# A causal matrix convolution: finishing a third of the outputs on ScalarE and GpSimd instead of VectorE

## The chip, the core and the metric

The kernel runs on one core of a Trainium2 chip. A core has five engines that run at once[...]: TensorE (PE, matmuls), VectorE (DVE), ScalarE (ACT), GpSimd (POOL) and SyncE (SP, which here only issues DMA). Matmul results land in PSUM; everything else lies in SBUF. The metric is the device time of one execution in microseconds (us).

## The reference

```python
B, S, D, K = 8, 4096, 512, 8
# x: [B, S, D] float32, kernel: [K, D, D] float32
out = 0
for k in range(K):
    shifted = x shifted down by k steps along S, zeros in front
    out += np.matmul(shifted, kernel[k])
```

Each output row is the sum of eight matrix products, of the row itself and its seven predecessors with eight 512 x 512 matrices.

## The kernel before

The 32768 rows are laid out as 128 runs (one on each partition) of 256 steps; an iteration handles 8 steps of every run, and there are 32. Within an iteration the kernel uses a fast (Karatsuba-like) scheme on the taps: three nodes, MID, LO and HI, each of nine 128 x 512 by 512 x 512 products. The MID node gives a common part `ms`, and the outputs of LO are its own sums plus `ms`, those of HI its own sums minus `ms`. Each node has two output tiles, b = 0 and 1, of 128 x 1024 float32 (two steps). The inputs of the products are sums of transposed inputs in bfloat16 (`XT`, `D1`, `D2`, `D21`, `D4`, `D41`, `D42`, `D421`), which VectorE prepares (`tt` is `nc.vector.tensor_tensor`). The engines' queues are taken in program order.

The helpers that matter here:

```python
def load(out, src):
    nc.gpsimd.dma_start(out=out, in_=src)          # float32 to bfloat16 on the way

def transpose_x(i, h):                             # half an iteration's input
    nc.sync.dma_start_transpose(out=XT[:, 4 * h:4 * h + 4, :]..., in_=xin[i, h]...)

def product(bank, comp, w, start):                 # four matmuls
    for c in range(DC):
        nc.tensor.matmul(bank, lhsT=comp[:, c * P:(c + 1) * P], rhs=w[:, c, :], ...)

mpool = tc.tile_pool(name="m", bufs=2)             # ms
ypool = tc.tile_pool(name="y", bufs=4)             # y
xpool = tc.tile_pool(name="x", bufs=2)             # xin

def node_a1(k): ...
    product(n.q[:, 1], ...)
    nc.scalar.copy(out=n.q[:, 0], in_=n.q[:, 1])                  # L244

def node_seed(n, b_):                                             # L256, L258
    n.p[b_] = pair((2 * n.k + b_) % 3)             # one of three PSUM pairs, in turn
    if b_ == LO: nc.scalar.copy(out=n.p[b_][:, 1], in_=n.q[:, 1])
    else:        nc.scalar.mul(out=n.p[b_][:, 1], in_=n.q[:, 1], mul=-1.0)

def node_dts(n): ...                                              # L262, ScalarE
def node_v(n, b_): product(n.p[b_][:, 1], ...)
def node_d(n, b_): ...            # VectorE: p[:, 0] from dts and p[:, 1]; L76, L272
def node_l(n, b_, j): product(n.p[b_][:, j], n.s[3][2 * b_ + j], W[n.a, b_, j], False)

def store(i, a, b_, y):
    nc.sync.dma_start(out=orr[:, t0:t0 + 2, :], in_=y)            # L282
```

The steady loop (the first six nodes are written out by hand; shown from the seventh on):

```python
for k, (i, a) in enumerate(order):            # (MID, LO, HI) of i = 2, 3, ... 31
    ...
    if a == MID and more: transpose_x(i + 1, 0)
    node_l(cur, 0, LO); node_l(cur, 0, HI)
    if nxt: node_a0(nxt); node_u(nxt)
    node_l(cur, 1, LO)
    node_e(cur, 0)                            # first output tile
    if nxt: node_seed(nxt, 0); node_seed(nxt, 1); node_dts(nxt)
    if a == MID:   prep_d421(LO); prep_d41(HI)
    elif a == LO:
        if more: prep_m()                     # reads the first half of the new XT
        prep_d421(HI)
    elif more:     prep_d41(LO); prep_d42(LO); prep_d21()
    if nxt:
        for b_ in range(2): node_v(nxt, b_); node_d(nxt, b_)
    if a == MID:   prep_d42(HI); prep_d27()
    elif more:     prep_d4(LO if a == LO else HI)     # HI: reads the second half of XT
    node_l(cur, 1, HI)
    if k + 2 < len(order): node_a1(k + 2)
    node_e(cur, 1)                            # second output tile
    if a == LO and more:
        transpose_x(i + 1, 1)
        if i + 2 < NIT: load_x(i + 2, 0); load_x(i + 2, 1)
```

Of the kernel before, what the change touches and what calls it, by code (L numbers as in the profile page):

```python
# [18 lines left out]
LO, HI, MID = 0, 1, 2  # L19
# [3 lines left out]
def kernel(  # L23
# [6 lines left out]
    nc = tc.nc  # L30
# [10 lines left out]
    ADD = mybir.AluOpType.add  # L41
    SUB = mybir.AluOpType.subtract
# [32 lines left out]
    def tt(o, a, b, op):  # L75
        nc.vector.tensor_tensor(out=o, in0=a, in1=b, op=op)  # L76
# [198 lines left out]
    ms = {}  # L275
# [4 lines left out]
    def store(i, a, b_, y):  # L280
        t0 = K * i + 4 * a + 2 * b_
        nc.sync.dma_start(out=orr[:, t0:t0 + 2, :], in_=y)  # L282
# [7 lines left out]
    def node_e(n, b_):  # L290
        p = n.p[b_]
        if n.k < 4:
            pool, name = ((mpool, "ms"), (ypool, "y"), (fpool, "f"), (ypool, "y"))[n.k]
            y = pool.tile([P, 2, D], f32, name=name)
            nc.scalar.copy(out=y, in_=p)  # L295
            first[n.i, n.a, b_] = y
        elif n.a == MID:
            ms[b_] = mpool.tile([P, 2, D], f32, name="ms")
            nc.scalar.copy(out=ms[b_], in_=p)  # L299
        else:  # L300
            y = ypool.tile([P, 2, D], f32, name="y")
            if b_ == HI and n.k == len(order) - 1:

                for j, eng in enumerate((nc.scalar, nc.sync)):
                    tt(y[:, j], p[:, j], ms[b_][:, j], ADD if n.a == LO else SUB)
                    eng.dma_start(out=orr[:, K * n.i + 4 * n.a + 2 * b_ + j, :], in_=y[:, j])
            else:
                tt(y, p, ms[b_], ADD if n.a == LO else SUB)
                store(n.i, n.a, b_, y)


# [108 lines left out]
    mid_dve(1, HI, HI)  # L420
    node_u(nodes[1])
    node_e(nodes[0], 0)
    prep_d27()
    mid_dve(2, HI, LO)
# [13 lines left out]
    mid_dve(2, HI, HI)  # L438
    mid_dve(2, HI, MID)
    node_e(nodes[0], 1)  # L440
    node_l(nodes[1], 0, HI)
    node_d(nodes[1], 1)
    prep_d421(HI)
    mid_acc(HI, LO)
    node_a1(2)
    node_l(nodes[1], 0, LO)
    node_e(nodes[1], 0)
    mid_dve(0, HI, HI)
    transpose_x(1, 1)
# [202 lines left out]
```

## Time and profile before

The median of two runs is 779.34 us (779.10 and 779.57). The profiled execution has a span of 777.3 us, with TensorE at its full granted clock throughout.

| engine | busy, us | share of span |
|---|---|---|
| TensorE matmuls | 766.8 | 99% |
| VectorE | 657.5 | 85% |
| ScalarE | 284.9 | 37% |
| GpSimd | 42.3 | 5% |

GpSimd's time is almost all issue of loads. The DMA queues of SyncE move 99.89 MB (stores and transposes), that of GpSimd 38.67 MB (loads).

In a group of instructions, the line reads: line of the kernel, engine, operation, what it writes and reads with shapes, count, then busy time in all, mean of one in ns, and the idle time of the engine just before with what ended it. `D` stands for all of the tiles D1 to D421, `pp` for the PSUM pairs. In a timeline a line begins with start and duration in us; neighbouring instructions of one kind are merged (x3), and `SPq` is a DMA issued from SyncE's queue. L76 is the helper `tt`, L89 the transpose, L80 the load.

### The profile page before, as it was taken

The page shows a single profiled execution, that of the slowest core. Times are in us where ns is not written, and L with a number is a line of the kernel's source. Part 1 is how long each engine was busy: PE and PEld are TensorE (multiplying, and loading weights), DVE is VectorE, ACT ScalarE, POOL GpSimd, SP SyncE. Part 2 cuts the span into 40 slices and gives each one's busy share as a digit, 9 for nine tenths or more (in the row PEclk, how much of TensorE's full clock was granted, in tenths as well). Part 3 has the DMA queues.
Part 4 walks back from the last instruction along what each step waited for, and adds up shares of the span by engine and source line. Part 5 has one row for each costly group of instructions (what it writes and reads, how often), then busy time and mean ns, then how long its engine had stood idle before and what let it go on. Part 6 is the DMA issues. An engine that isn't in the chain of part 4 may idle for free.

```text
span 777.3 us, 9450 instructions
## 1 busy us (share of the span) xinstructions
PE 766.8 (99%) x3584; PEld 347.3 (45%) x3584; DVE 657.5 (85%) x766; ACT 284.9 (37%) x462; POOL 42.3 (5%) x80
## 2 busy tenths in 40 slices
PE   7999999999999999999999999999999999999997
PEld 3444444444444444444444444444444444444443
DVE  4999988898888898888898888898888898888895
ACT  3553343333343333343333343333343333343332
POOL 4000000000000000000000000000000000000000
PEclk9999999999999999999999999999999999999999
DMA  9986878868786877787877878877697867687843
GB/s 199 211 125 170 226 185 178 208 159 190 164 199 163 197 172 189 164 198 169 194 171 187 164 174 190 207 162 188 163 187 176 207 158 190 165 186 179 204 133 121
DMA packets 159373, 139.42 MB, mean 179 GB/s; under 512 B 130144, under 2 KB 134240, under 8 KB 159200
## 3 DMA queue, kind: packets, MB, share of 16 engines
q1 hardware_dynamic: 145456, 99.89, 46.1%
q0 software_dynamic: 13728, 38.67, 31.6%
q8 instruction: 28, 0.46, 0.2%
q10 hardware_dynamic: 144, 0.26, 0.1%
q14 instruction: 17, 0.14, 0.1%
HBM read 77.33 MB, written 67.11 MB: 186 GB/s over the span
## 4 chain that ended last, share of the span: by engine, by line
PE 96%; DMA 2%; POOL 1%; ACT 0%; issue 0%; DVE 0%; DVEq 0%; POOLq 0%
PE pp L197 96%; DMA xin<-in_x_dram 2%; POOL w L80 0%; PE pp L186 0%; ACT y L295 0%; DVE y L76 0%; DVE pp L76 0%; POOL xin L80 0%; DVEq L647 0%; ACT pp L256 0%; ACT pp L244 0%; POOL XT L80 0%; PE pp L180 0%; POOL ident masks.py:199 0%; POOL ident masks.py:197 0%
## 5 line engine op out<-in xcount | busy, mean ns | idle before, releaser
L197 PE MATMUL pp<-w,D 128*128 128x512 bf16 x3280 | 715.5, 379 | 1.3 <-DVE w L76 0.9
L197 PEld LDWEIGHTS <-D 128*128 128x128 bf16 x3280 | 320.4, 98 | 389.8 <-issue 2.8
L76 DVE TENSOR_TENSOR D<-D 128x1024 bf16<-128x1024 bf16 (+1 forms) x252 | 228.2, 945 | 1.6 <-ACT D L353 1.6
L76 DVE TENSOR_TENSOR y<-pp,ms 128x1024 f32<-128x1024 f32 (+1 forms) x121 | 146.5, 1212 | 45.5 <-PE pp L197 45.4
L76 DVE TENSOR_TENSOR D<-XT 128x2048 bf16<-128x2048 bf16 (+2 forms) x153 | 142.1, 946 | 8.5 <-DMA XT<-xin 6.7
L244 ACT COPY pp<-pp 128x512 f32<-128x512 f32 x95 | 54.1, 570 | 256.0 <-PE pp L197 256.0
L256 ACT COPY pp<-pp 128x512 f32<-128x512 f32 x95 | 54.1, 570 | 170.6 <-PE pp L197 167.6
L76 DVE TENSOR_TENSOR pp<-dts,pp 128x512 f32<-128x512 f32 x95 | 65.5, 690 | 46.2 <-ACT dts L262 44.6
L299 ACT COPY ms<-pp 128x1024 f32<-128x1024 f32 x60 | 61.0, 1016 | 33.1 <-PE pp L197 33.1
L80 POOL DMA_DIRECT2D xin<-in_x_dram x64 | 34.2, 535 | 688.3 <-DMA XT<-xin 670.6
L272 DVE SCALAR_TENSOR_TENSOR pp<-pp,dts 128x512 f32<-128x512 f32 x95 | 65.9, 693 | 3.2
L262 ACT COPY dts<-pp 128x512 f32<-128x512 f32 x95 | 57.4, 604 | 2.0 <-PE pp L197 2.0
L258 ACT ACTIVATE pp<-pp 128x512 f32<-128x512 f32 x95 | 56.0, 589 | 1.2 <-DVE y L76 1.2
L197 PE MATMUL pp<-w,XT 128*128 128x512 bf16 x120 | 30.8, 379 | 0.0
L76 DVE TENSOR_TENSOR w<-w,w 128x2048 bf16<-128x2048 bf16 x18 | 21.6, 1219 | 0.4 <-DMA w<-in_kernel_dram 0.2
L197 PEld LDWEIGHTS <-XT 128*128 128x128 bf16 x120 | 11.7, 98 | 14.2
L180 PE MATMUL pp<-zero 128*128 128x512 bf16 x24 | 8.9, 505 | 2.4 <-DVE zero L145 1.2
L197 PE MATMUL pp<-w,w 128*128 128x512 bf16 x36 | 9.0, 379 | 1.3 <-ACT pp L244 0.7
L197 PE MATMUL pp<-w,F 128*128 128x512 bf16 x36 | 8.9, 379 | 0.0
L338 DVE MEMSET D<- 128x64 bf16 x2 | 0.2, 112 | 8.2 <-ACT D L351 7.7
L80 POOL DMA_DIRECT2D w<-in_kernel_dram x8 | 6.0, 766 | 0.8 <-DMA w<-in_kernel_dram 0.8
L197 PEld LDWEIGHTS <-w 128*128 128x128 bf16 x36 | 3.5, 97 | 5.8 <-issue 2.1
(55 smaller groups left out, 70.6 us busy)
## 6 DMA issues: line engine op xcount, KB each, us to landing
out_dram<-y SPq DMA_DIRECT2D x123, 512.0 KB, 3.5
xin<-in_x_dram POOLq DMA_DIRECT2D x64, 512.0 KB, 5.9
w<-in_kernel_dram POOLq DMA_DIRECT2D x8, 512.0 KB, 15.9
D<-in_x_dram SPq DMA_DIRECT2D x1, 1024.0 KB, 4.9
out_dram<-ms SPq DMA_DIRECT2D x2, 512.0 KB, 4.2
out_dram<-f SPq DMA_DIRECT2D x2, 512.0 KB, 3.7
XT<-xin SPq DMA_TRANSPOSE x61, 6.1
w<-w POOLq DMA_DIRECT2D x1, 512.0 KB, 9.9
```

The lines of the kernel that those rows point to most:

```text
L76: nc.vector.tensor_tensor(out=o, in0=a, in1=b, op=op)
L80: nc.gpsimd.dma_start(out=out, in_=src)
L180: nc.tensor.matmul(pw[:, h], lhsT=zero[:, 0:P], rhs=zero, start=True, stop=True)
L197: nc.tensor.matmul(bank, lhsT=comp[:, c * P:(c + 1) * P], rhs=w[:, c, :], start=start and c == 0, stop=c == DC - 1, skip_group_check=True)
L244: nc.scalar.copy(out=n.q[:, 0], in_=n.q[:, 1])
L256: nc.scalar.copy(out=n.p[b_][:, 1], in_=n.q[:, 1])
L258: nc.scalar.mul(out=n.p[b_][:, 1], in_=n.q[:, 1], mul=-1.0)
L262: nc.scalar.copy(out=n.dts, in_=n.q[:, 0])
L272: nc.vector.scalar_tensor_tensor(out=p[:, 0], in0=p[:, 1], scalar=-1.0, in1=n.dts, op0=MUL, op1=SUB)
L299: nc.scalar.copy(out=ms[b_], in_=p)
L338: nc.vector.memset(z[:, :, 0:D:G], 0.0)
```

## The change

The two outputs of every LO node no longer go through one VectorE addition that reads PSUM and writes SBUF. ScalarE copies the PSUM pair into the output tile, and GpSimd[...] adds `ms` to it in place. HI outputs stay on VectorE. The purpose is to take work off VectorE, the second busiest engine, and give it to two that have room; the sums are the same.

```diff
@@ node_e
                 for j, eng in enumerate((nc.scalar, nc.sync)):
                     tt(y[:, j], p[:, j], ms[b_][:, j], ADD if n.a == LO else SUB)
                     eng.dma_start(out=orr[:, K * n.i + 4 * n.a + 2 * b_ + j, :], in_=y[:, j])
+            elif n.a == LO:
+                nc.scalar.copy(out=y, in_=p)
+                nc.gpsimd.tensor_tensor(out=y, in0=y, in1=ms[b_], op=ADD)
+                store(n.i, n.a, b_, y)
             else:
-                tt(y, p, ms[b_], ADD if n.a == LO else SUB)
+                tt(y, p, ms[b_], SUB)
                 store(n.i, n.a, b_, y)
```

The order of work on TensorE and of issues on SyncE stays as it was. On GpSimd the two additions of a LO node come ahead of the two loads that are written after it.

## The prediction

> **What bounds the kernel now.** I read the page first: shares of busy time, then the chain of waits, then the groups. After that I read the timeline of one iteration in the steady part, because shares are averages over three different stages. The page, parts 1 and 4:
>
> ```profile
> PE 766.8 (99%) x3584; PEld 347.3 (45%) x3584; DVE 657.5 (85%) x766; ACT 284.9 (37%) x462; POOL 42.3 (5%) x80
> ...
> PE 96%; DMA 2%; POOL 1%; ACT 0%; issue 0%; DVE 0%; DVEq 0%; POOLq 0%
> ```
>
> TensorE is busy 99% and holds 96% of the chain. The detailed chain has one unbroken piece of 726.95 us and 3364 matmuls: 0.216 us each, 0.864 us for a product of four, 7.78 us for a node of nine products, 23.3 us for an iteration of MID, LO, HI. Every other engine works in its shadow, so taking work off VectorE buys nothing by itself; what counts is how much delay each helper may suffer before TensorE stops. The groups concerned, with shapes kept apart:
>
> ```profile
> L76 DVE TENSOR_TENSOR y<-pp,ms 128x1024 f32<-128x1024 f32 x119 | 145.2, 1221 | 45.0 <-PE pp L197 44.9
> L299 ACT COPY ms<-pp 128x1024 f32<-128x1024 f32 x60 | 61.0, 1016 | 33.1 <-PE pp L197 33.1
> ```
>
> Half of the first group moves; the second shows what a 128x1024 copy out of PSUM costs on ScalarE. Now the timeline of one iteration (start, duration, engine, line; in brackets the idle time before it). The LO node's products begin on TensorE at about 412.68: ScalarE's first seed (416.14) is released by the fourth product.
>
> ```profile
> 414.36 1.23 DVE L76 TENSOR_TENSOR y<-pp,ms 128x1024 f32<-128x1024 f32 x1 [1.29 <-PE pp L197]
> 414.60 0.53 POOL L80 DMA_DIRECT2D xin<-in_x_dram  x1 [9.46 <-DMA XT<-xin]
> ...
> 420.47 0.57 ACT L244 COPY pp<-pp 128x512 f32<-128x512 f32 x1 [2.75 <-PE pp L197]
> 420.70 1.22 DVE L76 TENSOR_TENSOR y<-pp,ms 128x1024 f32<-128x1024 f32 x1
> ...
> 422.38 3.26 SPq L89 DMA_TRANSPOSE XT<-xin  x1
> ...
> 423.28 2.95 DVE L76 TENSOR_TENSOR D<-D 128x1024 bf16<-128x1024 bf16 x3
> ...
> 426.15 0.69 DVE L76 TENSOR_TENSOR pp<-dts,pp 128x512 f32<-128x512 f32 x1
> ...
> 427.50 1.23 DVE L76 TENSOR_TENSOR D<-XT 128x2048 bf16<-128x2048 bf16 x1
> ...
> 428.64 1.22 DVE L76 TENSOR_TENSOR y<-pp,ms 128x1024 f32<-128x1024 f32 x1
> ...
> 431.63 0.57 ACT L256 COPY pp<-pp 128x512 f32<-128x512 f32 x1 [0.71 <-PE pp L197]
> ```
>
> 414.36 and 420.70 are the two outputs of LO. The transpose at 422.38 comes right after the second one's store, because the SyncE queue is taken in order. VectorE needs what it brings at 427.50 (prep_d4 of the upper half); behind that stands the second output of HI (428.64, done 429.86), which frees the PSUM pair that the seed at 431.63 overwrites. So the spare time in this line is 431.63 - 429.86 = 1.77 us. The kernel itself has tried it: at another iteration, where a transpose landed late,
>
> ```profile
> 242.67 1.23 DVE L76 TENSOR_TENSOR D<-XT 128x2048 bf16<-128x2048 bf16 x1 [1.79 <-DMA XT<-xin]
> ...
> 245.12 0.57 ACT L256 COPY pp<-pp 128x512 f32<-128x512 f32 x1 [0.76 <-PE pp L197]
> ```
>
> 1.79 us of delay reached VectorE and TensorE just did not stop. Anything beyond that is paid on the path.
>
> [...] The trace has no GpSimd arithmetic of this kind to compare; VectorE takes 1.22 us for the version that reads PSUM. [...] a transpose suffers beside a load: with no load near, the one issued at 422.38 had landed by 427.50 (5.1 us at most); the one issued at 407.06, 2.45 us after a load, released the next load only at 414.60 (7.5 us).
>
> **The change part by part.** It removes 60 VectorE additions (30 LO nodes with two outputs), 60 x 1.22 = 73 us, leaving about 584 us of VectorE. It adds 60 ScalarE copies of 1.016 us, 61 us, making 346 us (44%), and 60 GpSimd additions of an estimated 2.3 us, 138 us. Nothing moves on TensorE. The stores keep their places in the SyncE queue but now wait for GpSimd. The two loads of each iteration stand behind both GpSimd additions in GpSimd's own queue.
>
> ScalarE has room. The first copy runs at 414.4 to 415.4, before the seed of 416.14; the second after the copy of 420.47, from 421.0 to 422.0, before its next work at 423.86. PSUM is freed at 422.0 where it was 421.92. Nothing is lost here.
>
> GpSimd's second addition then runs 422.05 to 424.35 where VectorE had finished at 421.92: the LO output is complete 2.4 us later. Its store and the transpose behind it go with it: the transpose is issued at 424.8. At the same moment, 424.4, GpSimd issues the load that used to go at 414.60, so load and transpose now start together[...]. The transpose lands after 5.1 us if unhurt, at 429.9, and after some 7.5 us if it is slowed as above, at 432.3. VectorE's second HI output ends 2.36 us later (429.86 - 427.50 in the trace): 432.3 or 434.7. The seed takes 0.57 more and a semaphore, so the first v product of the next LO can start at 432.9 or 435.3; it was due at 412.68 + 7.78 + 7.78 + 5 products x 0.864 = 432.5. TensorE loses 0.4 or 2.8 us in each iteration. I take 2.4, since I expect the collision in most of them.
>
> The lock adds to that. The three D additions due at 423.28 wait for GpSimd until 424.4; node_d then ends at 428.0, and the MID node wants it at 428.2: it just fits. GpSimd's first addition (from 415.45) competes with prep_m and the D421 addition; as the other transpose is issued behind the delayed HI store, it lands later too, and GpSimd will often be first. Then 2.9 us of D additions and 0.7 us of node_d follow 417.8, to 421.4, where the HI node starts at 420.4: up to 1.0 us lost. I take 0.6.
>
> The sum is 2.4 + 0.6 = 3.0 us in each of 29 iterations that still load a successor (the last LO has no transpose behind it), 87 us. The saved VectorE time shortens nothing on the path. 779.3 + 87 = 866 us.
>
> **The rivals.** (a) Nothing changes: the 1.77 us of spare time swallow the delay, as in the late transpose above. This asks for an addition under 1.7 us or a transpose that is quicker than now; the estimates speak against it. It would give 775 to 790. (b) A gain through VectorE's relief: VectorE at 85% looks like a near bound, but TensorE's chain has no wait on it in the steady part, so at most the small start-up and end waits are in play, under 5 us, and those are not touched. (c) GpSimd itself becomes slow: if it often waits for the port behind VectorE's D additions, an addition lasts 4 to 5 us instead of 2.3, and the store, transpose and load go with it; each us more is about 29 us. That would give 900 to 950. (d) ScalarE as the bound: at 44%, with gaps at both places where the copies fall, I hold this unlikely; it would show as seeds that wait for a copy.
>
> **Range and chances.** With a clean transpose and no lock loss, 29 x 0.4 gives 791, and a slightly slow addition already passes 800. With the full collision and the full lock loss, 29 x 3.8 gives 890; with GpSimd delayed by half a us besides, 905. The range for 8 in 10 is 815 to 908. Slower by over 2% (above 795) needs 0.55 us lost in an iteration: 0.92. Within 2%: 0.07. Faster: 0.01.
>
> **What would show each step right or wrong.** TensorE's busy time should stay while its idle time grows by the loss, and its waits should name ScalarE's seeds (L256) in the MID nodes, which in turn wait for VectorE's HI output, and that for the DMA transpose: VectorE's wait on XT should grow from 6.7 us to well over 60. The stores of LO should wait for GpSimd, and the transposes after them land in 7 us or more. GpSimd's additions should last about 2.3 us each, in step with D additions that start late. I am wrong on the transpose if VectorE's wait on it stays small; wrong on the lock if D additions run during GpSimd's; wrong altogether if TensorE's chain stays unbroken.

## The result, and the profile after

The changed kernel takes 989.17 us (median of two, 987.74 and 990.61) against 779.34: a ratio of 1.269, interval 1.265 to 1.274. That is 209.8 us, or 7.2 us for each of the 29 iterations that transpose a successor's input in the LO node. The prediction said 866, with 908 at the top of its range. The outputs that moved are 60 of the 128 output tiles, so nearly half and not the third of the title. The page of the changed kernel, busy times, the clock granted to TensorE in 40 slices (tenths), and the chain by engine:

```profile
PE 830.8 (84%) x3513; PEld 362.0 (37%) x3584; DVE 636.6 (65%) x706; ACT 343.4 (35%) x522; POOL 192.7 (20%) x140
...
PEclk9999999998899888998888988889888898888989
...
PE 49%; DMA 30%; DVE 13%; issue 5%; ACT 2%; POOL 0%; another core or an unknown queue 0%; DVEq 0%; ACTq 0%; POOLq 0%
```

TensorE held 96% of the chain and now holds 49%; DMA has 30%. TensorE's busy time also grew, by 64.0 us, with the same matmuls to do, and its mean granted clock is 0.909. The waits (who waited for whom: us in all, times, longest):

```profile
DVE D L76 <- DMA XT<-xin: 185.1, 58, 6.9
ACT pp L256 <- DVE y L76: 159.8, 29, 6.8
PE pp L197 <- ACT pp L256: 135.6, 30, 6.1
```

The same three waits in the kernel before:

```profile
DVE D L76 <- DMA XT<-xin: 6.7, 6, 1.8
ACT pp L256 <- DVE y L76: 0.8, 1, 0.8
PE pp L197 <- ACT pp L256: 0.7, 1, 0.7
```

Read upwards: TensorE waits for the seed, the seed for VectorE's HI output, and VectorE for the transpose, 29 times or more each. The 135.6 us of waiting and the 64.0 us of slower matmuls make 199.6 of the 208.7 us by which the span grew (986.0 against 777.3). One iteration in the timeline:

```profile
510.46 0.15 PEld L197 LDWEIGHTS <-D 128*128 128x128 bf16 x1 [0.27 <-issue]
...
510.89 0.15 PEld L197 LDWEIGHTS <-D 128*128 128x128 bf16 x1 [0.28 <-issue]
511.32 0.15 PEld L197 LDWEIGHTS <-D 128*128 128x128 bf16 x1 [0.28 <-issue]
...
524.08 2.35 POOL L309 TENSOR_TENSOR y<-y,ms 128x1024 f32<-128x1024 f32 x1 [4.15 <-issue]
...
525.26 3.99 DVE L76 TENSOR_TENSOR D<-D 128x1024 bf16<-128x1024 bf16 x3
...
526.37 0.57 POOL L80 DMA_DIRECT2D xin<-in_x_dram  x1
...
526.96 6.88 SPq L89 DMA_TRANSPOSE XT<-xin  x1
...
537.35 1.23 DVE L76 TENSOR_TENSOR D<-XT 128x2048 bf16<-128x2048 bf16 x1 [6.89 <-DMA XT<-xin]
...
538.50 1.22 DVE L76 TENSOR_TENSOR y<-pp,ms 128x1024 f32<-128x1024 f32 x1
...
539.80 0.57 ACT L256 COPY pp<-pp 128x512 f32<-128x512 f32 x1 [6.83 <-DVE y L76]
...
540.42 15.70 PE L197 MATMUL pp<-w,D 128*128 128x512 bf16 x63 [5.97 <-ACT pp L256]
```

GpSimd's second addition ends at 526.43. Its load goes out at 526.37 and the transpose at 526.96, 0.59 us apart. The transpose brings its data after 10.3 us, where it was 5.1 before; VectorE waits 6.89 us, the seed goes at 539.80 and TensorE has stood still for 5.97 us. Of the 28 transposes of this place that have a load beside them, 19 landed in 8.6 to 9.0 us, three in 9.2 to 9.3 and six in 9.9 to 10.3; TensorE stood 4.1 to 4.8 us after the first 19 and up to 6.1 after the others. The first three lines show what follows such a gap: weight loads, one for each matmul, come every 0.43 us instead of every 0.216. The granted clock is 0.50 in the first 2 us of work after this gap (540.30 to 542.30) and 1.00 again from 544.30 on.

The groups of arithmetic on GpSimd and of VectorE's D additions, and the last of them in the kernel before:

```profile
L76 DVE TENSOR_TENSOR D<-D 128x2048 bf16<-128x2048 bf16 x123 | 158.0, 1303 | 0.0
L309 POOL TENSOR_TENSOR y<-y,ms 128x1024 f32<-128x1024 f32 x60 | 151.2, 2519 | 453.5 <-ACT y L308 343.4 <-issue 110.1
L76 DVE TENSOR_TENSOR D<-D 128x1024 bf16<-128x1024 bf16 x127 | 112.0, 921 | 1.6 <-ACT D L357 1.6
```

```profile
L76 DVE TENSOR_TENSOR D<-D 128x1024 bf16<-128x1024 bf16 x127 | 81.8, 682 | 1.6 <-ACT D L353 1.6
```

GpSimd's additions take 2.34 to 2.35 us where no D addition runs beside them (11 of the 60) and 2.52 us on average. VectorE's D additions of 128x1024 went from 682 to 921 ns. 29 of them began while a GpSimd addition was running: every one ended after it, and they took 1.37 to 2.00 us where the other 98 took 0.68 to 0.69. So the two exclude each other, and the time in which an instruction waits is counted as its own. The 28 HI outputs that began during a GpSimd addition, and read PSUM for one operand, did not wait: 1.22 to 1.23 us, where 29 others without one took 1.22. "Lock" and "port" in the recorded texts are names for this exclusion, and what lies behind it no run shows.

### The profile page after: what moved, and what is told of

Read it like the earlier page. It is cut to its first block, busy times and chain, and to the rows that moved or that the text cites. A ratio compares the mean times of both kernels' runs of the same rounds, so it can differ in the third digit from the quotient of the medians.

```text
span 986.0 us, 9495 instructions
## 1 busy us (share of the span) xinstructions
PE 830.8 (84%) x3513; PEld 362.0 (37%) x3584; DVE 636.6 (65%) x706; ACT 343.4 (35%) x522; POOL 192.7 (20%) x140
## 4 chain that ended last, share of the span: by engine, by line
PE 49%; DMA 30%; DVE 13%; issue 5%; ACT 2%; POOL 0%; another core or an unknown queue 0%; DVEq 0%; ACTq 0%; POOLq 0%
PE pp L197 49%; DMA XT<-xin 28%; DVE y L76 7%; DVE D L76 6%; DMA xin<-in_x_dram 2%; ACT pp L256 2%; POOL w L80 0%; DVE pp L76 0%; PE pp L186 0%; ACT y L295 0%; POOL xin L80 0%; DVEq L76 0%; DVEq L651 0%; ACT pp L244 0%
## 5 line engine op out<-in xcount | busy, mean ns | idle before, releaser
L197 PE MATMUL pp<-w,D 128*128 128x512 bf16 x3214 | 780.1, 402 | 142.0 <-ACT pp L256 135.0
L197 PEld LDWEIGHTS <-D 128*128 128x128 bf16 x3280 | 335.2, 102 | 580.9 <-issue 227.9
L76 DVE TENSOR_TENSOR D<-D 128x1024 bf16<-128x1024 bf16 (+1 forms) x252 | 269.3, 1108 | 1.6 <-ACT D L357 1.6
L76 DVE TENSOR_TENSOR D<-XT 128x2048 bf16<-128x2048 bf16 (+2 forms) x153 | 144.5, 961 | 185.1 <-DMA XT<-xin 185.1
L309 POOL TENSOR_TENSOR y<-y,ms 128x1024 f32<-128x1024 f32 x60 | 151.2, 2519 | 453.5 <-ACT y L308 343.4
L244 ACT COPY pp<-pp 128x512 f32<-128x512 f32 x95 | 54.1, 570 | 318.4 <-PE pp L197 310.2
L76 DVE TENSOR_TENSOR y<-pp,ms 128x1024 f32<-128x1024 f32 (+1 forms) x61 | 73.4, 1204 | 42.4 <-PE pp L197 40.8
L308 ACT COPY y<-pp 128x1024 f32<-128x1024 f32 x60 | 61.0, 1017 | 6.9 <-PE pp L197 6.7
```

The costliest lines, as they stand in the source:

```text
L309: nc.gpsimd.tensor_tensor(out=y, in0=y, in1=ms[b_], op=ADD)
```

## The experiments

Four theories. A, collision: the load, held back by GpSimd's additions, starts together with the transpose and slows it. B, queue: the transpose is issued late because it stands behind a store that waits for a slow addition. C, exclusion: VectorE's D additions and GpSimd's additions wait for each other, and that delay reaches TensorE. D, clock: after the gap TensorE runs at half speed. A ratio is always to the kernel before, measured on the same chip.

### Taking the collision away: the load goes first

```diff
+        if a == LO and i + 2 < NIT:
+            load_x(i + 2, 0)
         node_l(cur, 0, LO)
@@
             if i + 2 < NIT:
-                load_x(i + 2, 0)
                 load_x(i + 2, 1)
```

> The changed kernel, with the first of an iteration's two loads written ahead of the LO node's two GpSimd additions instead of behind them. Theory A (the load, held back by the additions, starts together with the transpose and slows it): the second-half transpose lands in 5 to 6 us again instead of about 10, TensorE loses at most 1 us an iteration and its clock stays full; 785 to 815 us. Theory B (the transpose is late because it stands behind a store that waits for a 2.5 us addition): nothing of that changes, the time stays above 900. Theory C[...]: above 900 too.

836.64 us, ratio 1.075 (1.072 to 1.077): 152.5 us of the 209.8 are gone by moving one load. The chain of waits of this run shows the second-half transposes (start, duration until it released the next step):

```profile
451.88 4.97 DMA XT<-xin
...
476.80 5.00 DMA XT<-xin
...
526.64 4.95 DMA XT<-xin
```

They land in 5.0 us again (23 of 28 in 4.4 to 5.0, the other five in 6.0 to 6.4), and TensorE's clock is 0.994. The time is above the expected 785 to 815: TensorE still waits 23.8 us for node_d and 15.7 us for seeds, because the transpose is issued late and D additions stand behind GpSimd's.

### Taking the queue away: the transpose goes ahead of the second store

```diff
-        node_e(cur, 1)
         if a == LO and more:
             transpose_x(i + 1, 1)
+        node_e(cur, 1)
```

> The changed kernel, with the second-half transpose written ahead of the LO node's second store in SyncE's queue; loads still behind the additions. Theory B: the transpose is issued when its buffer is free, about 1 us earlier than in the kernel before, and the loss disappears; 779 to 790. Theory A: the load still comes some 3 us into the transpose and slows the rest of it; landing 6 to 8 us, but from an earlier start, so 780 to 810. Theory C: above 900.

813.68 us, 1.044 (1.043 to 1.046): 175.5 us gone. The transpose now starts about 2.1 us before the load:

```profile
512.64 1.93 SPq L89 DMA_TRANSPOSE XT<-xin  x1
...
514.77 0.57 POOL L80 DMA_DIRECT2D xin<-in_x_dram  x1
...
517.45 0.53 POOL L80 DMA_DIRECT2D xin<-in_x_dram  x1 [2.10 <-DMA XT<-xin]
```

The last line is the second load, which waits for the transpose to land. That is 4.3 us after its start here and 4.2 to 4.5 in 25 of 28 iterations (6.6 to 6.8 in the other three), less than the 5.0 of the kernel before. So this run takes away the collision together with the wait in the queue, and does not tell A from B. What is left is another wait, before the HI node. Its timeline:

```profile
505.12 2.34 POOL L309 TENSOR_TENSOR y<-y,ms 128x1024 f32<-128x1024 f32 x1 [11.60 <-ACT y L308]
505.50 3.65 DVE L76 TENSOR_TENSOR D<-XT 128x1024 bf16<-128x1024 bf16 x2 [2.82 <-DMA XT<-xin]
...
509.07 1.21 DVE L76 TENSOR_TENSOR D<-D 128x2048 bf16<-128x2048 bf16 x1
...
510.94 2.75 PE L197 MATMUL pp<-w,D 128*128 128x512 bf16 x12 [0.95 <-DVE pp L76]
```

The first-half transpose lands just after GpSimd's first addition has begun, and prep_m, 1.82 us in the kernel before, takes 3.65. TensorE waits 0.95 us for node_d in nearly every iteration.

### Both moves

The two diffs above together.

> Both moves together. If A and B hold all of the loss, 777 to 783, the same as before the change[...]. If C holds a part, that part is left: each us lost in an iteration is 29 us.

787.55 us, 1.011 (1.009 to 1.012). So A and B together hold 201.6 of the 209.8 us. Either move alone removes most of it, because either alone ends the collision: 5.0 and 4.3 us to landing in the two runs above. With no collision on either side, the step from the early load to both moves is what the transpose's place behind the store costs, 49.1 us (836.64 against 787.55), with whatever of C goes with it. VectorE still waits for GpSimd, now mostly out of the path:

```profile
512.39 2.61 POOL L309 TENSOR_TENSOR y<-y,ms 128x1024 f32<-128x1024 f32 x1 [0.38 <-ACT y L308]
512.72 3.37 DVE L76 TENSOR_TENSOR D<-D 128x2048 bf16<-128x2048 bf16 x1
```

The D421 addition, 1.22 us by itself, ends at 516.09, 1.09 us after GpSimd's end at 515.00: it stood still until GpSimd was done.

### ScalarE's copy without GpSimd

```diff
                 nc.scalar.copy(out=y, in_=p)
-                nc.gpsimd.tensor_tensor(out=y, in0=y, in1=ms[b_], op=ADD)
+                tt(y, y, ms[b_], ADD)
```

> ScalarE copies the LO outputs out of PSUM as in the change, but VectorE adds ms in SBUF, so GpSimd does no arithmetic. If GpSimd's part is what costs, 778 to 785 (the second addition ends about 1.3 us later than in the kernel before, inside the 1.77 us of spare time). If the extra copy on ScalarE or the later freeing of PSUM costs, above 800.

789.51 us, 1.013 (1.012 to 1.015), a little above what I expected and far from the loss. The waits show why:

```profile
ACT pp L256 <- DVE y L76: 15.9, 10, 2.5
PE pp L197 <- ACT pp L256: 7.3, 11, 1.6
```

The second output is complete 1.3 us later than before (2.76 us after the start of ScalarE's L244 copy against 1.45), so of the 1.77 us of spare time under 0.5 are left; where a transpose takes 6 to 7 us instead of 5.1, which happened in the kernel before too, the seed is now late. ScalarE's copies cost no more than that.

### A short addition

GpSimd adds 32 of 1024 columns; the rest of that sum is left out.

```diff
-                nc.gpsimd.tensor_tensor(out=y, in0=y, in1=ms[b_], op=ADD)
+                nc.gpsimd.tensor_tensor(out=y[:, 0, 0:32], in0=y[:, 0, 0:32], in1=ms[b_][:, 0, 0:32], op=ADD)
```

> The changed kernel, with GpSimd adding only 32 of the 1024 columns (so most of the sum in the LO outputs is left out): its additions last a few tenths of a us. If the length of the addition is the cost (B, C), the delay behind ScalarE's copy is gone and the time returns to 780 to 790. If the point is that load and transpose are set free at the same moment (A), they still start together, some 2 us earlier than in the changed kernel; the transpose still takes 8 to 10 us, and 2 to 4 us an iteration are lost: 840 to 900.

928.64 us, 1.191 (1.188 to 1.195). With additions of 0.4 us on average 149 us of the loss remain: the length of the addition was not the main thing. The timeline:

```profile
495.30 0.25 POOL L309 TENSOR_TENSOR y<-y,ms 128x32 f32<-128x32 f32 x1 [6.34 <-issue]
...
495.80 0.57 POOL L80 DMA_DIRECT2D xin<-in_x_dram  x1 [0.24 <-issue]
...
496.08 7.29 SPq L89 DMA_TRANSPOSE XT<-xin  x1
...
506.99 1.22 DVE L76 TENSOR_TENSOR D<-XT 128x2048 bf16<-128x2048 bf16 x1 [6.35 <-DMA XT<-xin]
```

Load and transpose start 0.28 us apart and the transpose takes 10.9 us; 19 of the 28 landed in 8.8 to 9.8 us and nine in 10.6 to 11.8. The time is somewhat more than I expected, since TensorE's gaps of 2.6 to 5.4 us also slow the clock (0.938).

### Held loads in the kernel before

Here VectorE completes all outputs as before, and GpSimd does two additions of the same size for nothing, ahead of the loads.

```diff
                 store(n.i, n.a, b_, y)
+                if n.a == LO:
+                    nc.gpsimd.tensor_tensor(
+                        out=F21.bitcast(f32).rearrange("p (a b) d -> p a (b d)", b=2),
+                        in0=y, in1=ms[b_], op=ADD)
```

> The kernel before (VectorE completes the outputs), with two GpSimd additions of the same size per LO node, whose result nobody reads, ahead of the loads. The stores and the transpose are not held back in SyncE's queue; the load is[...]. Theory A alone: the load now starts about 2 us after the second-half transpose and slows it to 6 to 8 us; 0.3 to 2 us an iteration lost, 785 to 840. If only the queue (B) matters: 779 to 783. If the port (C) matters by itself: above 830 with the transposes landing in 5 us.

885.68 us, 1.136 (1.134 to 1.138), more than any theory said. The second-half transposes land in 7.1 to 8.6 us with the load 2.0 us behind them, and TensorE waits in three places an iteration: for the seed; for node_d of MID, since the three D additions before it stand behind GpSimd's addition (4.29 us for 2.95); and for node_d of HI, since the first-half transpose lands late too. This run mixes A and C, so a second one takes the arithmetic out: GpSimd copies one column of each second LO output, and the loads wait for that.

```diff
                 store(n.i, n.a, b_, y)
+                if n.a == LO and b_ == HI:
+                    nc.gpsimd.tensor_copy(out=F21.bitcast(f32)[:, 0, 0:1], in_=y[:, 0, 0:1])
```

> The kernel before, in which GpSimd copies one column of each second LO output and does nothing else, so that the loads are held until that output is there, about 0.5 us before the second-half transpose is issued. No addition on GpSimd,[...] no delay in SyncE's queue. Theory A by itself: the transpose lands after 8.5 to 9 us instead of 5.1, of which 1.8 us are spare; 2 us an iteration are lost, 830 to 850. If the cost in the earlier run with held loads (885.7 us) came from the port: below 795.

893.91 us, 1.147 (1.141 to 1.153). But for a one-column copy of 0.18 us, only the time of a load differs from the kernel before: it goes 0.1 us after the second-half transpose where it went 7.8 us ahead of it, and that costs 114 us:

```profile
506.47 0.18 POOL L311 COPY F<-y 128x1 f32<-128x1 f32 x1 [15.10 <-DVE y L76]
...
506.87 6.49 SPq L89 DMA_TRANSPOSE XT<-xin  x1
506.95 0.53 POOL L80 DMA_DIRECT2D xin<-in_x_dram  x1 [0.30 <-issue]
...
515.85 1.23 DVE L76 TENSOR_TENSOR D<-XT 128x2048 bf16<-128x2048 bf16 x1 [3.92 <-DMA XT<-xin]
...
518.91 3.40 PE L197 MATMUL pp<-w,D 128*128 128x512 bf16 x15 [1.97 <-ACT pp L256]
```

A landing of 9.0 us costs 2.0 us here, as expected. But in 10 of 28 iterations TensorE stands 3.2 to 3.9 us, in nine of them after a landing of 10.2 to 10.5. After 8 of these 10 gaps, and after 9 of the 18 of about 2 us, a slow stretch of TensorE follows (clock 0.958). The waits for seeds, 72.6 us, and the slower matmuls, 36.8 us, are the whole of the longer span (886.8 us against 777.3). That is where the expected 830 to 850 fell short.

### Filling the gap

24 matmuls that nobody uses, 5.2 us, in the MID node where TensorE stood idle:

```diff
+        if a == MID:
+            keep = pair((2 * nxt.k + 1) % 3)
+            for t in range(24):
+                nc.tensor.matmul(keep[:, t % 2], lhsT=ident, rhs=W[LO, LO, LO][:, 0, :],
+                                 start=True, stop=True)
         if nxt:
             node_seed(nxt, 0)
```

> The changed kernel, with 24 matmuls without use, 5.2 us, put where TensorE otherwise stands idle for 5 to 6 us before the first v product in each MID node. Theory D (after such a gap TensorE runs its next matmuls at half speed, and the lost 2 us go round the loop of waits): TensorE does 150 us more of work and the kernel becomes faster, about 989 - 29 x 2 = 930. Without D the time stays at 985 to 1000.

959.75 us, 1.231 (1.229 to 1.233). With 150 us more work for TensorE the kernel is 29 us faster, and the clock is 0.999. D is right in kind, but half of what I expected came back. The unused work might have been the limit, so I took 14 of them (the same diff with 14 for 24).

> The changed kernel with 14 unused matmuls (3.0 us) in the gap, where an earlier run had 24 (5.2 us) and left no gap at all, so that the unused work had itself become the bound (23.3 + 5.2 + 0.95 = 29.5 us an iteration, and 29.6 were measured). Theory D (a gap of 2.6 us or more is followed by about 2 us of lost time at half clock, inside the loop of waits): with a rest of 1 to 2 us the clock stays full and the whole 2 us come back; 920 to 935 us. If the slow stretch was hidden behind other waits, about 960 or more.

961.56 us, 1.234 (1.231 to 1.237), clock 0.980: the same. (The 2.6 us of the expectation are the shortest gap in the run with the short addition; 23 of the 28 gaps there were followed by a slow stretch, not all.) The chain of waits says where the rest went:

```profile
500.41 8.22 DMA XT<-xin
...
512.95 1.90 PE pp L197 x8
...
517.36 8.78 DMA XT<-xin
```

In this run both transposes of an iteration are in the chain. The first-half one takes 8.2 us, prep_m then stands behind GpSimd's first addition (2.49 us for 1.82), and TensorE waits 0.96 us for node_d. My reading, which no run isolates, is that in the changed kernel the slow stretch of TensorE hides this wait. What the two fillings gave back is 29.4 and 27.6 us, so of 64 us of slower matmuls about 28 are net.

### The exclusion by itself

The early-transpose run with GpSimd's first addition cut to 64 columns (the rest of that sum is left out):

```diff
+                w_ = 512 if b_ else 32
+                nc.gpsimd.tensor_tensor(out=y[:, :, 0:w_], in0=y[:, :, 0:w_],
+                                        in1=ms[b_][:, :, 0:w_], op=ADD)
```

> The run with the early transpose (813.7 us), in which GpSimd's first addition of each LO node is cut to 64 of 1024 columns (the rest of that sum is left out); the second stays whole, so the load is released as late as before. Theory C (what was left there, 0.95 us an iteration before the HI node, is VectorE's D addition standing behind GpSimd's first one[...]): 784 to 790. If the late landing of the first-half transpose alone is the cause, it stays at 808 to 815.

785.92 us, 1.008 (1.007 to 1.010). 27.8 of the 34.3 us that were left there were the first addition's: C, 0.95 us an iteration.

### What remains, and whether anything is to be gained

Both moves, and only the second output over ScalarE and GpSimd:

```diff
-            elif n.a == LO:
+            elif n.a == LO and b_ == HI:
```

> Load and transpose both moved ahead (787.5 us), and of each LO node only the second output goes over ScalarE and GpSimd; the first is completed by VectorE as in the kernel before. If the remaining 8 us come from GpSimd's first addition[...]: 778.5 to 781, and in spite of 37 us less work on VectorE nothing is gained on the kernel before. If they come from the second addition or from the copies: 785 or more.

781.86 us, 1.0036 (1.0023 to 1.0049). The steady part has no gap any more: TensorE ends at 773.05, as before at 772.81. The 2.4 us are at the very end:

```profile
770.77 2.35 POOL L309 TENSOR_TENSOR y<-y,ms 128x1024 f32<-128x1024 f32 x1 [19.55 <-ACT y L308]
...
773.15 0.81 SPq L282 DMA_DIRECT2D out_dram<-y  x2
```

The last LO output is complete only at 773.12, so its store and the one queued behind it go out together when TensorE is already done. Last, the two moves without the change:

> The kernel before (VectorE completes all outputs) with the two moves alone: first load ahead of the LO outputs, second-half transpose ahead of the second store. TensorE is the bound, so nothing can be gained: 778.5 to 780. If the 2.4 us that the run with only the second output moved lost on the kernel before (781.9) come from the moves themselves, this run shows them too: 781 to 783. If it stays at 779.4, they come from the second output's way over ScalarE and GpSimd.

779.24 us, 0.9998 (0.9990 to 1.0006): no gain, and the moves cost nothing. No version tried beats the kernel before, which is bound by TensorE.

## Why the prediction was wrong

**What bounds the kernel, the spare time, the chain.** Right. TensorE lost its time exactly in the line that the prediction drew, and the relation holds: it gave a loss of 0.4 us for a landing of 5.1 and 2.8 for 7.5, so 4.2 for 8.9 and 5.7 for 10.4; the trace has 4.5 and 5.97.

**The step that failed: "after some 7.5 us if it is slowed as above".** The size of the collision. I took it from a transpose that starts 2.45 us after a load. In the changed kernel they start within 0.6 us, and the transpose takes 8.6 to 10.3 us to land. Then I weighed even that down, to 2.4 us of loss where the average is 135.6 / 29 = 4.7. The run with the early load shows 5.0 us for the same transpose, and the run with a held load and nothing else 8.8 to 10.5, so it is the load's time that makes the difference.

**A term that was missing: the clock.** The prediction held that TensorE's busy time would stay, and its sum had no line for matmuls at half speed: 64.0 us of busy time, 2.2 us an iteration, about 28 us net by the filled gaps. In the changed kernel all 28 gaps, 4.1 us and longer, are followed by 7 to 13 weight loads about 0.43 us apart. Shorter gaps can do the same: in the held-load run without additions 9 of the 18 gaps of about 2 us were followed by such a stretch. My own loss of 2.4 us, and the upper case of 2.8, thus asked for the term.

**The lock.** The prediction took it as given; no trace of the kernel before shows it, and the changed kernel does. Right that the D additions of the MID node would just fit, and right on the HI node, "up to 1.0 us", wherever TensorE arrives there in time: 0.95 us in the run with the early transpose. In the changed kernel itself it cost nothing there (TensorE waited 1.0 us in all for node_d), since TensorE was late; the 0.6 us an iteration were not to be added to a loss that already makes TensorE late.

**ScalarE and GpSimd's times.** Right: 343.4 us against 346, additions of 2.35 us free and 2.52 on average against 2.3, which was my estimate, with no trace behind it. VectorE's 584 became 636.6, mostly because waiting counts as busy: the 35 D additions that began during a GpSimd addition hold 42.7 of the 52.6 us.

**The rivals.** (a), (b) and (d) fell, as held. (c) named an addition of 4 to 5 us as the way past 900; the kernel went past 900 without it, and its longest addition took 3.39 us.

Not settled: why a transpose under the same conditions takes either about 8.9 or about 10.3 us (and without a load 5.0 or 6.8), and by what means a load slows a transpose. Nor is it settled what part the store has that goes out just ahead of the transpose. With the load 2.0 us behind it and that store ahead, in the first run with held loads, the transpose lands in 7.1 to 8.6 us; with the load 2.1 us behind it and the store behind it too, in the run with the early transpose, mostly in 4.3. No run starts load and transpose together without that store.

## What to carry to other kernels

When work moves to another engine, look first at what else stands in that engine's queue and in the queues that wait for it: here a load behind two additions and a transpose behind a store cost more than the arithmetic. Place loads and transposes by the time at which they start, not only by when they are needed, and size a collision from two transfers that start as yours will, not from two that start 2.45 us apart. A helper engine at 85% under a TensorE at 99% is no bound, so relieving it can gain nothing and can lose its spare time.

## What the runs showed of the hardware that I had not expected

One load of 512 KB in each iteration, moved from 7.8 us ahead of a transpose to 0.1 us behind its start, made the kernel before 14.7% slower, with only a one-column copy added. TensorE can be given 150 us of useless matmuls and the kernel becomes 29 us faster. In the traces of the changed kernel and of four runs (early load, short addition, held load without arithmetic, 14 unused matmuls), the slow stretch followed every gap of TensorE of 3.9 us or more, about 40 of the 57 between 2.0 and 3.6 us, and none that was shorter. The exclusion works in both directions: the D421 addition stood until GpSimd's end (3.37 us for 1.22), and a GpSimd addition that found VectorE at work mostly took 3.12 us for 2.35 in the run with the early transpose.
